# RMSNorm with GELU: tiles taken one at a time in a hand-written order, half of the squares moved from ScalarE to VectorE

One core of one Trainium2 chip. The metric is the device time of one execution in microseconds, median of the fast runs. All runs in this study were in the fast state, with a granted clock of 1.00 in each.

## The reference

`x` is 8 x 1024 x 2048 float32, `gamma` has 2048 elements. Every row is normalised, scaled and passed through GELU:

```python
rms = np.sqrt(np.mean(x ** 2, axis=-1, keepdims=True) + eps)
out = gamma * x / rms
return 0.5 * out * (1 + np.tanh(np.sqrt(2 / np.pi) * (out + 0.044715 * out ** 3)))
```

67.1 MB have to come in and 67.1 MB have to go out. There are 32 tiles of 256 rows (128 partitions x 2 rows x 2048), 2.1 MB each way.

## The kernel before

Loads are issued by SyncE, stores by ScalarE's queue. For a group of two tiles ScalarE squares and sums each row into `ssq`, VectorE multiplies by gamma into a bf16 tile `w`; then VectorE works out 1/rms for the group by a bit trick and two Newton steps (10 small operations); then ScalarE applies GELU with 1/rms as its scale.

```python
SG = 2                                             # tiles in a group
xpool = tc.tile_pool(name="xpool", bufs=5)         # (cut: enter_context)
wpool = tc.tile_pool(name="wpool", bufs=4)
ypool = tc.tile_pool(name="ypool", bufs=3)
sqpool = tc.tile_pool(name="sqpool", bufs=2, space=PSUM)
...
for G in group_sizes:
    for j in range(G):
        nc.sync.dma_start(out=x_tile, in_=...)
        for t in range(T):
            nc.scalar.activation(out=sq_scratch, in_=x_tile[:, t, :], func=AF.Square,
                                 accum_out=ssq[:, j * T + t: j * T + t + 1])
        nc.vector.tensor_mul(out=w_tile, in0=x_tile, in1=gamma_bc)
    # 10 small VectorE operations on 128 x 4: ssq -> mtile -> ... -> rr
    for j in range(G):
        for t in range(T):
            nc.scalar.activation(out=y_tile[:, t, :], in_=w_tiles[j][:, t, :],
                                 func=AF.Gelu_apprx_tanh, scale=rr[:, ...])
        nc.scalar.dma_start(out=..., in_=y_tile)
```

The order in which VectorE and ScalarE issue these is not the order written. A scheduler in the framework places them, and in the built program VectorE's multiplies stand ahead of the statistics: the multiply of tile 31 (290.34 us in the trace), for one, stands before the statistics of tiles 28 and 29 (294.68 us), so that four multiplied tiles (the four `w` buffers) wait for theirs. "Statistics" here are the small operations that make 1/rms. This order turns out to matter more than which engine does the squares.

Of the kernel before, what the change touches and what calls it, by code (L numbers as in the profile page):

```python
# [1 line left out]

# [4 lines left out]

FP32 = mybir.dt.float32
BF16 = mybir.dt.bfloat16
I32 = mybir.dt.int32  # L10
AF = mybir.ActivationFunctionType
ALU = mybir.AluOpType

_RSQRT_MAGIC = float(0x5F3759DF)


@with_exitstack
def kernel(
    ctx: ExitStack,
    tc: tile.TileContext,  # L20
    x: bass.AP,
    gamma: bass.AP,
    eps: float,
    out: bass.AP,
):
    nc = tc.nc
    P = nc.NUM_PARTITIONS

    xf = x.flatten_outer_dims()
    of = out.flatten_outer_dims()  # L30
    N, H = xf.shape

    T = 2
    rows_per_tile = P * T
    assert N % rows_per_tile == 0
    ntiles = N // rows_per_tile
    SG = 2
    COLS = SG * T

    singles = ctx.enter_context(tc.tile_pool(name="singles", bufs=1))  # L40
    xpool = ctx.enter_context(tc.tile_pool(name="xpool", bufs=5))
    wpool = ctx.enter_context(tc.tile_pool(name="wpool", bufs=4))
    ypool = ctx.enter_context(tc.tile_pool(name="ypool", bufs=3))
    sqpool = ctx.enter_context(tc.tile_pool(name="sqpool", bufs=2, space=bass.MemoryType.PSUM))
    stats = ctx.enter_context(tc.tile_pool(name="stats", bufs=4))

    gamma_sb = singles.tile([P, H], FP32)
    nc.sync.dma_start(out=gamma_sb, in_=gamma.partition_broadcast(P))
    gamma_bc = gamma_sb.rearrange("p (o h) -> p o h", o=1).to_broadcast([P, T, H])

    inv_h = 1.0 / float(H)
    eps_f = float(eps)

    group_sizes = [SG] * (ntiles // SG)
    rem = ntiles % SG
    if rem:
        group_sizes.append(rem)

    base = 0
    for G in group_sizes:  # L60
        ssq = stats.tile([P, COLS], FP32)
        mtile = stats.tile([P, COLS], FP32)
        y0i = stats.tile([P, COLS], I32)
        t0 = stats.tile([P, COLS], FP32)
        t1 = stats.tile([P, COLS], FP32)
        u0 = stats.tile([P, COLS], FP32)
        y1 = stats.tile([P, COLS], FP32)
        t2 = stats.tile([P, COLS], FP32)
        t3 = stats.tile([P, COLS], FP32)
        u1 = stats.tile([P, COLS], FP32)  # L70
        rr = stats.tile([P, COLS], FP32)

        ncols = G * T
        w_tiles = []
        for j in range(G):
            i = base + j
            r0 = i * rows_per_tile
            x_tile = xpool.tile([P, T, H], FP32)
            nc.sync.dma_start(
                out=x_tile,  # L80
                in_=xf[r0:r0 + rows_per_tile, :].rearrange("(p t) h -> p t h", t=T),
            )

            for t in range(T):
                sq_scratch = sqpool.tile([P, H], FP32)
                nc.scalar.activation(  # L86
                    out=sq_scratch,
                    in_=x_tile[:, t, :],
                    func=AF.Square,
                    accum_out=ssq[:, j * T + t: j * T + t + 1],  # L90
                )

            w_tile = wpool.tile([P, T, H], BF16)
            nc.vector.tensor_mul(out=w_tile, in0=x_tile, in1=gamma_bc)  # L94
            w_tiles.append(w_tile)

        sg = slice(0, ncols)
        nc.vector.tensor_scalar(  # L98
            out=mtile[:, sg], in0=ssq[:, sg], scalar1=inv_h, scalar2=eps_f,
            op0=ALU.mult, op1=ALU.add,  # L100
        )
        nc.vector.tensor_scalar(  # L102
            out=y0i[:, sg], in0=mtile[:, sg].bitcast(I32), scalar1=-0.5,
            scalar2=_RSQRT_MAGIC,
            op0=ALU.mult, op1=ALU.add,
        )
        y0f = y0i.bitcast(FP32)
        nc.vector.tensor_mul(out=t0[:, sg], in0=y0f[:, sg], in1=y0f[:, sg])  # L108
        nc.vector.tensor_mul(out=t1[:, sg], in0=t0[:, sg], in1=mtile[:, sg])  # L109
        nc.vector.tensor_scalar(  # L110
            out=u0[:, sg], in0=t1[:, sg], scalar1=-0.5, scalar2=1.5,
            op0=ALU.mult, op1=ALU.add,
        )
        nc.vector.tensor_mul(out=y1[:, sg], in0=y0f[:, sg], in1=u0[:, sg])  # L114
        nc.vector.tensor_mul(out=t2[:, sg], in0=y1[:, sg], in1=y1[:, sg])  # L115
        nc.vector.tensor_mul(out=t3[:, sg], in0=t2[:, sg], in1=mtile[:, sg])  # L116
        nc.vector.tensor_scalar(  # L117
            out=u1[:, sg], in0=t3[:, sg], scalar1=-0.5, scalar2=1.5,
            op0=ALU.mult, op1=ALU.add,
        )  # L120
        nc.vector.tensor_mul(out=rr[:, sg], in0=y1[:, sg], in1=u1[:, sg])  # L121

        for j in range(G):
            i = base + j
            r0 = i * rows_per_tile
            y_tile = ypool.tile([P, T, H], FP32)
            for t in range(T):
                nc.scalar.activation(  # L128
                    out=y_tile[:, t, :],
                    in_=w_tiles[j][:, t, :],  # L130
                    func=AF.Gelu_apprx_tanh,
                    scale=rr[:, j * T + t: j * T + t + 1],
                )
            nc.scalar.dma_start(
                out=of[r0:r0 + rows_per_tile, :].rearrange("(p t) h -> p t h", t=T),
                in_=y_tile,
            )

        base += G


# [1 line left out]
_INS = ['x', 'gamma', 'eps']  # L143
_OUTS = [((8, 1024, 2048), 'float32')]
#: Inputs that are plain numbers.
_NUMBERS = {'eps': 9.999999747378752e-06}


# [26 lines left out]
```

## Time and profile before

| | before |
|---|---|
| median | 330.06 us (329.39 to 330.27, 13 runs) |
| span of the profiled run | 328.0 us |
| VectorE / ScalarE busy | 166.5 us (51%) / 247.0 us (75%) |
| moved | 135.3 MB, 412 GB/s over the span |
| moved in the middle (100 to 256 us, four windows of 39 us) | 430 to 432 GB/s |
| transfers idle in the tail (the two "holes") | 3.0 + 5.5 us |

The busy shares are averages over the span. The rate in the middle against the rate over the span tells more: something is lost outside the middle. The lines are in the prediction.

### The profile page before, as it was taken

The page shows a single profiled execution, that of the slowest core. Times are in us where ns is not written, and L with a number is a line of the kernel's source. Part 1 is how long each engine was busy: PE and PEld are TensorE (multiplying, and loading weights), DVE is VectorE, ACT ScalarE, POOL GpSimd, SP SyncE. Part 2 cuts the span into 40 slices and gives each one's busy share as a digit, 9 for nine tenths or more (in the row PEclk, how much of TensorE's full clock was granted, in tenths as well). Part 3 has the DMA queues.
Part 4 walks back from the last instruction along what each step waited for, and adds up shares of the span by engine and source line. Part 5 has one row for each costly group of instructions (what it writes and reads, how often), then busy time and mean ns, then how long its engine had stood idle before and what let it go on. Part 6 is the DMA issues. An engine that isn't in the chain of part 4 may idle for free.

```text
span 328.0 us, 586 instructions
## 1 busy us (share of the span) xinstructions
DVE 166.5 (51%) x192; ACT 247.0 (75%) x194; POOL 0.2 (0%) x4
## 2 busy tenths in 40 slices
DVE  0698476557544365654447554455754446551100
ACT  1589719996976949589594977949498694968890
POOL 0000000000000000000000000000000000000000
DMA  8999999999999999999999999999999999996938
GB/s 314 438 424 372 428 434 428 436 428 437 424 440 421 440 424 440 424 438 426 438 426 438 426 438 424 436 426 436 427 436 428 434 428 433 430 434 262 388 160 352
DMA packets 9364, 135.30 MB, mean 412 GB/s; under 512 B 1040, under 2 KB 1040, under 8 KB 1040
## 3 DMA queue, kind: packets, MB, share of 16 engines
q1 hardware_dynamic: 4752, 68.16, 49.1%
q10 hardware_dynamic: 4608, 67.11, 47.8%
q14 instruction: 4, 0.03, 0.0%
HBM read 68.16 MB, written 67.11 MB: 412 GB/s over the span
## 4 chain that ended last, share of the span: by engine, by line
DMA 43%; ACT 24%; DVE 19%; issue 12%; SPq 0%; DVEq 0%
DMA x_tile<-in_x_dram 37%; ACT y_tile L128 19%; DVE w_tile L94 13%; DMA out_dram<-y_tile 6%; ACT sq_scratch L86 5%; DVE u L117 1%; DVE y0i L102 1%; DVE u L110 1%; DVE t L108 1%; DVE t L116 1%; DVE y L114 1%; DVE rr L121 1%; DVE t L109 1%; DVE t L115 1%; DVE mtile L98 0%
## 5 line engine op out<-in xcount | busy, mean ns | idle before, releaser
L94 DVE TENSOR_TENSOR w_tile<-x_tile,gamma_sb 128x4096 bf16<-128x4096 f32 x32 | 141.4, 4425 | 126.4 <-DMA x_tile<-in_x_dram 58.4
L128 ACT ACTIVATE y_tile<-w_tile,rr 128x2048 f32<-128x2048 bf16 x64 | 123.1, 1991 | 62.5 <-DVE rr L121 62.1
L86 ACT ACTIVATE sq_scratch<-x_tile 128x2048 f32<-128x2048 f32 x64 | 118.9, 1858 | 9.5 <-DMA x_tile<-in_x_dram 9.5
L86 ACT ACTIVATION_READ_ACCUMULATOR sq_scratch<-x_tile 128x1 f32 x64 | 11.9, 186 | 0.0
L98 DVE TENSOR_SCALAR mtile<-ssq 128x4 f32<-128x4 f32 x16 | 2.6, 164 | 14.1 <-ACT sq_scratch L86 14.1
L117 DVE TENSOR_SCALAR u<-t 128x4 f32<-128x4 f32 x16 | 2.7, 170 | 0.6
L110 DVE TENSOR_SCALAR u<-t 128x4 f32<-128x4 f32 x16 | 2.7, 170 | 0.6
L102 DVE TENSOR_SCALAR y0i<-mtile 128x4 int32<-128x4 int32 x16 | 2.7, 170 | 0.5
L108 DVE TENSOR_TENSOR t<-y0i 128x4 f32<-128x4 f32 x16 | 2.6, 163 | 0.5
L109 DVE TENSOR_TENSOR t<-t,mtile 128x4 f32<-128x4 f32 x16 | 2.6, 162 | 0.5
L116 DVE TENSOR_TENSOR t<-t,mtile 128x4 f32<-128x4 f32 x16 | 2.6, 162 | 0.6
L115 DVE TENSOR_TENSOR t<-y 128x4 f32<-128x4 f32 x16 | 2.6, 161 | 0.6
L114 DVE TENSOR_TENSOR y<-y0i,u 128x4 f32<-128x4 f32 x16 | 2.6, 162 | 0.5
L121 DVE TENSOR_TENSOR rr<-y,u 128x4 f32<-128x4 f32 x16 | 2.6, 161 | 0.5
L86 ACT ACT_TABLE_LOAD x1 | 1.3, 1283 | 0.7 <-PEq L156 0.7
L128 ACT ACT_TABLE_LOAD x1 | 1.3, 1283 | 0.0
L156 POOL MEMSET const-uint8-127<- 128x1 uint8 x1 | 0.1, 103 | 0.0
L156 POOL MEMSET const-bfloat16-1.0<- 128x1 bf16 x1 | 0.1, 102 | 0.0
L156 POOL MEMSET const-float32-0.0<- 128x1 f32 x1 | 0.1, 99 | 0.2 <-issue 0.2
L156 POOL MEMSET const-float32-1.0<- 128x1 f32 x1 | 0.1, 99 | 0.0
## 6 DMA issues: line engine op xcount, KB each, us to landing
x_tile<-in_x_dram SPq DMA_DIRECT2D x32, 2048.0 KB, 23.5
out_dram<-y_tile ACTq DMA_DIRECT2D x32, 2048.0 KB, 19.3
gamma_sb<-in_gamma_dram SPq DMA_DIRECT2D x1, 1024.0 KB, 4.8
```

The costliest lines, as they stand in the source:

```text
L86: nc.scalar.activation(out=sq_scratch, in_=x_tile[:, t, :], func=AF.Square, accum_out=ssq[:, j * T + t: j * T + t + 1],)
L94: nc.vector.tensor_mul(out=w_tile, in0=x_tile, in1=gamma_bc)
L102: nc.vector.tensor_scalar(out=y0i[:, sg], in0=mtile[:, sg].bitcast(I32), scalar1=-0.5, scalar2=_RSQRT_MAGIC, op0=ALU.mult, op1=ALU.add,)
L108: nc.vector.tensor_mul(out=t0[:, sg], in0=y0f[:, sg], in1=y0f[:, sg])
L109: nc.vector.tensor_mul(out=t1[:, sg], in0=t0[:, sg], in1=mtile[:, sg])
L110: nc.vector.tensor_scalar(out=u0[:, sg], in0=t1[:, sg], scalar1=-0.5, scalar2=1.5, op0=ALU.mult, op1=ALU.add,)
L114: nc.vector.tensor_mul(out=y1[:, sg], in0=y0f[:, sg], in1=u0[:, sg])
L115: nc.vector.tensor_mul(out=t2[:, sg], in0=y1[:, sg], in1=y1[:, sg])
L116: nc.vector.tensor_mul(out=t3[:, sg], in0=t2[:, sg], in1=mtile[:, sg])
L117: nc.vector.tensor_scalar(out=u1[:, sg], in0=t3[:, sg], scalar1=-0.5, scalar2=1.5, op0=ALU.mult, op1=ALU.add,)
L121: nc.vector.tensor_mul(out=rr[:, sg], in0=y1[:, sg], in1=u1[:, sg])
L128: nc.scalar.activation(out=y_tile[:, t, :], in_=w_tiles[j][:, t, :], func=AF.Gelu_apprx_tanh, scale=rr[:, j * T + t: j * T + t + 1],)
```

## The change

Its intent is to balance the two engines and shorten the path of a tile. One of a tile's two rows of squares goes to VectorE as a fused multiply-and-sum; tiles are handled one at a time; one Newton step goes; there are four y buffers for three; and a hand order replaces the scheduler's on VectorE and ScalarE, with the next tile's square ahead of this tile's GELUs. The core, with cuts:

```diff
-    SG = 2
-    COLS = SG * T
+    COLS = 2
-    ypool = ... bufs=3      sqpool = ... bufs=2
+    ypool = ... bufs=4      sqpool = ... bufs=1
+    # DVE and ACT issue in the order written here.
+    ctx.enter_context(tc.manual_schedule(
+        engines={mybir.EngineType.DVE, mybir.EngineType.Activation}))
+    def front(i):                                   # (cut: load, tiles)
+        nc.vector.tensor_tensor_reduce(
+            out=dve_sq_scratch, in0=x_tile[:, 0, :], in1=x_tile[:, 0, :],
+            scale=inv_h, scalar=eps_f, op0=ALU.mult, op1=ALU.add, accum_out=m[:, 0:1])
+        nc.scalar.activation(out=act_sq_scratch, in_=x_tile[:, 1, :], func=AF.Square,
+                             scale=sqrt_inv_h, accum_out=s)
+        nc.vector.tensor_mul(out=w, in0=x_tile, in1=gamma_bc)
+        ...                                         # 6 small operations on 128 x 2 (10 on 128 x 4 before)
+    def back(i):
+        for t in range(T):
+            nc.scalar.activation(out=y[:, t, :], in_=ws[i][:, t, :],
+                                 func=AF.Gelu_apprx_tanh, scale=rrs[i][:, t:t + 1])
+        nc.scalar.dma_start(out=o, in_=y)
+    for i in range(ntiles):
+        front(i)
+        if i:
+            back(i - 1)
+    back(ntiles - 1)
```

More of the change, by code (lines that the diff above doesn't have):

```diff
@@ L34 @@
     rows_per_tile = P * T
-    assert N % rows_per_tile == 0
     ntiles = N // rows_per_tile
-    SG = 2
-    COLS = SG * T
+    COLS = 2
     singles = ctx.enter_context(tc.tile_pool(name="singles", bufs=1))
@@ L42 @@
     wpool = ctx.enter_context(tc.tile_pool(name="wpool", bufs=4))
-    ypool = ctx.enter_context(tc.tile_pool(name="ypool", bufs=3))
-    sqpool = ctx.enter_context(tc.tile_pool(name="sqpool", bufs=2, space=bass.MemoryType.PSUM))
+    ypool = ctx.enter_context(tc.tile_pool(name="ypool", bufs=4))
+    sqpool = ctx.enter_context(tc.tile_pool(name="sqpool", bufs=1, space=bass.MemoryType.PSUM))
     stats = ctx.enter_context(tc.tile_pool(name="stats", bufs=4))
@@ L51 @@
     inv_h = 1.0 / float(H)
+    sqrt_inv_h = float(inv_h ** 0.5)
     eps_f = float(eps)
-    group_sizes = [SG] * (ntiles // SG)
-    rem = ntiles % SG
-    if rem:
-        group_sizes.append(rem)
-    base = 0
-    for G in group_sizes:
-        ssq = stats.tile([P, COLS], FP32)
-        mtile = stats.tile([P, COLS], FP32)
-        y0i = stats.tile([P, COLS], I32)
-        t0 = stats.tile([P, COLS], FP32)
-        t1 = stats.tile([P, COLS], FP32)
-        u0 = stats.tile([P, COLS], FP32)
-        y1 = stats.tile([P, COLS], FP32)
-        t2 = stats.tile([P, COLS], FP32)
-        t3 = stats.tile([P, COLS], FP32)
-        u1 = stats.tile([P, COLS], FP32)
-        rr = stats.tile([P, COLS], FP32)
-        ncols = G * T
-        w_tiles = []
-        for j in range(G):
-            i = base + j
-            r0 = i * rows_per_tile
-            x_tile = xpool.tile([P, T, H], FP32)
-            nc.sync.dma_start(
-                out=x_tile,
-                in_=xf[r0:r0 + rows_per_tile, :].rearrange("(p t) h -> p t h", t=T),
-            )
-            for t in range(T):
-                sq_scratch = sqpool.tile([P, H], FP32)
-                nc.scalar.activation(
-                    out=sq_scratch,
-                    in_=x_tile[:, t, :],
-                    func=AF.Square,
-                    accum_out=ssq[:, j * T + t: j * T + t + 1],
-                )
-            w_tile = wpool.tile([P, T, H], BF16)
-            nc.vector.tensor_mul(out=w_tile, in0=x_tile, in1=gamma_bc)
-            w_tiles.append(w_tile)
-        sg = slice(0, ncols)
-        nc.vector.tensor_scalar(
-            out=mtile[:, sg], in0=ssq[:, sg], scalar1=inv_h, scalar2=eps_f,
-            op0=ALU.mult, op1=ALU.add,
-        )
-        nc.vector.tensor_scalar(
-            out=y0i[:, sg], in0=mtile[:, sg].bitcast(I32), scalar1=-0.5,
-            scalar2=_RSQRT_MAGIC,
-            op0=ALU.mult, op1=ALU.add,
-        )
-        y0f = y0i.bitcast(FP32)
-        nc.vector.tensor_mul(out=t0[:, sg], in0=y0f[:, sg], in1=y0f[:, sg])
-        nc.vector.tensor_mul(out=t1[:, sg], in0=t0[:, sg], in1=mtile[:, sg])
-        nc.vector.tensor_scalar(
-            out=u0[:, sg], in0=t1[:, sg], scalar1=-0.5, scalar2=1.5,
-            op0=ALU.mult, op1=ALU.add,
-        )
-        nc.vector.tensor_mul(out=y1[:, sg], in0=y0f[:, sg], in1=u0[:, sg])
-        nc.vector.tensor_mul(out=t2[:, sg], in0=y1[:, sg], in1=y1[:, sg])
-        nc.vector.tensor_mul(out=t3[:, sg], in0=t2[:, sg], in1=mtile[:, sg])
-        nc.vector.tensor_scalar(
-            out=u1[:, sg], in0=t3[:, sg], scalar1=-0.5, scalar2=1.5,
-            op0=ALU.mult, op1=ALU.add,
-        )
-        nc.vector.tensor_mul(out=rr[:, sg], in0=y1[:, sg], in1=u1[:, sg])
-        for j in range(G):
-            i = base + j
-            r0 = i * rows_per_tile
-            y_tile = ypool.tile([P, T, H], FP32)
-            for t in range(T):
-                nc.scalar.activation(
-                    out=y_tile[:, t, :],
-                    in_=w_tiles[j][:, t, :],
-                    func=AF.Gelu_apprx_tanh,
-                    scale=rr[:, j * T + t: j * T + t + 1],
-                )
-            nc.scalar.dma_start(
-                out=of[r0:r0 + rows_per_tile, :].rearrange("(p t) h -> p t h", t=T),
-                in_=y_tile,
-            )
-        base += G
@@ new lines, with rows @@
+    act_sq_scratch = sqpool.tile([P, H], FP32)
+    dve_sq_scratch = singles.tile([P, H], FP32)
+    ctx.enter_context(tc.manual_schedule(
+        engines={mybir.EngineType.DVE, mybir.EngineType.Activation}))
+    xs, ws, rrs = {}, {}, {}
+    def rows(i):
+        return slice(i * rows_per_tile, (i + 1) * rows_per_tile)
+    def front(i):
+        x_tile = xpool.tile([P, T, H], FP32, name="x_tile")
+        nc.sync.dma_start(out=x_tile, in_=xf[rows(i), :].rearrange("(p t) h -> p t h", t=T))
+        m = stats.tile([P, COLS], FP32, name="mtile")
+        s = stats.tile([P, 1], FP32, name="s_act")
+        nc.vector.tensor_tensor_reduce(
[3 more added lines that the diff above has]
+                             scale=sqrt_inv_h, accum_out=s)
+        w = wpool.tile([P, T, H], BF16, name="w_tile")
+        nc.vector.tensor_mul(out=w, in0=x_tile, in1=gamma_bc)
+        y0i = stats.tile([P, COLS], I32, name="y0i")
+        t0 = stats.tile([P, COLS], FP32, name="t0")
+        t1 = stats.tile([P, COLS], FP32, name="t1")
+        u0 = stats.tile([P, COLS], FP32, name="u0")
+        rr = stats.tile([P, COLS], FP32, name="rr")
+        nc.vector.tensor_scalar(out=m[:, 1:2], in0=s, scalar1=eps_f, scalar2=None, op0=ALU.add)
+        nc.vector.tensor_scalar(out=y0i, in0=m.bitcast(I32), scalar1=-0.5,
+                                scalar2=_RSQRT_MAGIC, op0=ALU.mult, op1=ALU.add)
+        y0f = y0i.bitcast(FP32)
+        nc.vector.tensor_mul(out=t0, in0=y0f, in1=y0f)
+        nc.vector.tensor_mul(out=t1, in0=t0, in1=m)
+        nc.vector.tensor_scalar(out=u0, in0=t1, scalar1=-0.5, scalar2=1.5, op0=ALU.mult, op1=ALU.add)
+        nc.vector.tensor_mul(out=rr, in0=y0f, in1=u0)
+        ws[i], rrs[i] = w, rr
@@ L143 @@
+    def back(i):
+        y = ypool.tile([P, T, H], FP32, name="y_tile")
+        o = of[rows(i), :].rearrange("(p t) h -> p t h", t=T)
+        for t in range(T):
+            nc.scalar.activation(out=y[:, t, :], in_=ws[i][:, t, :], func=AF.Gelu_apprx_tanh,
+                                 scale=rrs[i][:, t:t + 1])
+        nc.scalar.dma_start(out=o, in_=y)
[4 more added lines that the diff above has]
+    back(ntiles - 1)
 _INS = ['x', 'gamma', 'eps']
```

## The prediction

> **What bounds the kernel now.** I read the page from the top: busy time of each engine, then the slices, then the costly rows.
>
> ```profile
> DVE 166.5 (51%) x192; ACT 247.0 (75%) x194; POOL 0.2 (0%) x4
> ...
> DVE  0698476557544365654447554455754446551100
> ACT  1589719996976949589594977949498694968890
> ...
> DMA  8999999999999999999999999999999999996938
> GB/s 314 438 424 372 428 434 428 436 428 437 424 440 421 440 424 440 424 438 426 438 426 438 426 438 424 436 426 436 427 436 428 434 428 433 430 434 262 388 160 352
> ```
>
> No compute engine is full: ScalarE is busy 75% of the span, VectorE 51%. The DMA line is at 9 in every slice from the second to the 36th and drops only in the last four (6, 9, 3, 8; the span is 328.0 us, so a slice is 8.2 us). So the kernel has two stages: some 298 us in which the transfers are the limit, and a tail in which they wait for work. The three large groups:
>
> ```profile
> L94 DVE TENSOR_TENSOR w_tile<-x_tile,gamma_sb 128x4096 bf16<-128x4096 f32 x32 | 141.4, 4425 | 126.4 <-DMA x_tile<-in_x_dram 58.4
> L128 ACT ACTIVATE y_tile<-w_tile,rr 128x2048 f32<-128x2048 bf16 x64 | 123.1, 1991 | 62.5 <-DVE rr L121 62.1
> L86 ACT ACTIVATE sq_scratch<-x_tile 128x2048 f32<-128x2048 f32 x64 | 118.9, 1858 | 9.5 <-DMA x_tile<-in_x_dram 9.5
> ```
>
> ScalarE's 62 us of waiting for `rr` look tempting, but they lie in the stage in which the transfers never pause, so they cost nothing there. What the transfers leave unused is read from the windows of the tail (length, busy time of DVE, ACT and POOL, clock, DMA share, GB/s):
>
> ```profile
> 296.00:298.00 2.00, 0.53 (x4) 1.33 (x1) 0.00 (x0) 1.00 0.82 352
> 298.00:300.00 2.00, 0.00 (x0) 2.00 (x2) 0.00 (x0) 1.00 0.06 25
> 300.00:302.00 2.00, 0.00 (x0) 2.00 (x2) 0.00 (x0) 1.00 0.31 131
> 302.00:304.00 2.00, 0.00 (x0) 2.00 (x2) 0.00 (x0) 1.00 1.15 483
> ...
> 310.00:312.00 2.00, 1.64 (x10) 0.02 (x1) 0.00 (x0) 1.00 0.62 262
> 312.00:314.00 2.00, 0.01 (x1) 1.96 (x2) 0.00 (x0) 1.00 0.00 0
> 314.00:316.00 2.00, 0.00 (x0) 2.00 (x3) 0.00 (x0) 1.00 0.00 0
> 316.00:318.00 2.00, 0.00 (x0) 2.00 (x2) 0.00 (x0) 1.00 0.61 262
> ```
>
> With one-microsecond windows the edges are about 298.1 to 301.1 and 311.0 to 316.5: two holes, 3.0 and 5.5 us, 8.5 us in all, and ScalarE busy in nearly all of both. The timeline says why: groups of two tiles. The last group's statistics come only after all its squares on ScalarE, which stand behind the previous group's GELUs.
>
> ```profile
> 300.59 0.34 ACTq L134 DMA_DIRECT2D out_dram<-y_tile  x1
> ...
> 310.05 0.17 DVE L98 TENSOR_SCALAR mtile<-ssq 128x4 f32<-128x4 f32 x1 [13.42 <-ACT sq_scratch L86]
> ...
> 312.04 5.79 ACT L128 ACTIVATE y_tile<-w_tile,rr 128x2048 f32<-128x2048 bf16 x3 [2.02 <-DVE rr L121]
> 315.97 0.34 ACTq L134 DMA_DIRECT2D out_dram<-y_tile  x1
> ```
>
> The last input tile is multiplied from 290.34 us on and the program ends at 328.0, so about 38 us follow the last load.
>
> [...] in the middle, groups of two tiles start their GELUs at 140.24 and 159.67 us, 19.43 us apart, in which 4 x 2.097 MB = 8.39 MB move, 432 GB/s. So I expect nothing from the middle. [...] loads alone land 4.9 us apart (multiplies released at 10.51 and 15.33), beside stores 9.7 us apart (31.82 and 41.55). [...]
>
> **The change part by part.**
> - *Squares.* Half of the 64 squares leave ScalarE: 32 x (1858 + 186 - 93 overlap) ns, some 62 us. VectorE gets 32 fused multiply-and-sum operations of 2048 elements[...].
> - *Statistics.* 10 small operations per two tiles become 6 per tile, so 12 per two; they start 0.20 us apart in the timeline, so 1.2 us per tile. One Newton step goes; that is accuracy, not time.
> - *VectorE per tile*: 2.3 + 0.1 + 4.4 + 1.2 = 8.0 us. *ScalarE per tile*: 1.95 (square) + 3.9 (two GELUs at 1.9 us from start to start) + about 1 for issuing the store before the next square = 7. Both lie under the 9.7 us that the transfers need per tile, so the middle stays bound by the transfers, with 1.7 us of room on VectorE.
> - *Order.* square(i+1) stands before gelu(i) on ScalarE, so a store is issued about 16 us after its tile landed: 9.7 until the next lands, 2.0 square, 3.9 GELU, 0.1. The group of two is gone.
> - *Buffers.* Four y tiles for three. gelu(i) needs store(i-4) done; I count below that it is, by over 10 us. The PSUM scratch has one buffer; it is written by ScalarE alone, in order.
>
> Now the whole run. Tile 0 lands at 10.4 as before. VectorE: to 12.9 sum, 17.3 multiply, 18.5 statistics. ScalarE: square(0), square(1) to 17.3, table load 1.3, gelu(0) 18.7 to 22.6, store issued 22.7 (it was 25.59), data moving from an estimated 23.5. By then 1 + (23.5 - 10.4)/4.88 = 3.7 tiles are loaded: the loads lead the stores by 3.7 tiles. VectorE makes a tile every 8.0 us and a store takes 9.7 beside a load, so the store queue does not run dry, and with both queues full and equal shares the lead stays 3.7. Store k then runs from 23.5 + 9.72k, and the last load lands at T = 23.5 + (32 - 3.7) x 9.72 = 298.6. (gelu(i) starts at about 9 + 9.72i, store(i-4) ends at 23.5 + 9.72(i-3) = -6 + 9.72i: 15 us to spare.)
>
> Tail, from T: 3.7 stores are left; alone each takes 5.0 us (two took 301.1 to 311.0). Stores 28 and 29, already issued, run to T+8.5. Store 30: square(31) 2.0, gelu(30) 3.9, issued T+6.1, in time; it runs to T+13.5. Store 31: VectorE 8.0, gelu(31) 4.0, issued T+12.1, moving T+12.9, just in time; ends T+18.5. The old run ends 1.4 us after the last byte (326.6 to 328.0), so the span is 298.6 + 18.5 + 1.4 = 318.5. A second way: the old transfers were active from 2.1 to 326.6 less 8.5, 316.0 us; with no hole at all 2.1 + 316.0 + 1.4 = 319.5. The median is 2.1 us above the span, so 320.6 to 321.6; I take 321.2, which is 2.7% off.
>
> **The rivals.**
> - *VectorE becomes the bound.* [...] it takes about 4.4 us instead of 2.3, a tile 10.1, over the 9.7 of the transfers: 10.4 + 32 x 10.1 + gelu 4.0 + store 5.8 + 1.4 = 345 span, 347 us, slower by 5%. [...] About 6%.
> - *The hole closes only in part.* The tail has only 0.5 us of slack before store 31. A dispatch gap behind each store issue, or a store queue that ran dry in the middle so that the loads got further ahead (the old lead at the last load was about 5.5 tiles), leaves 2 to 4 us of idle: 323 to 325. For it: the old run did let its loads get ahead. Against it: the holes came of work in groups, and at T only one square and four GELUs are left. About 20%.
> - *Nothing gained*, as ScalarE's relief was hidden behind transfers anyway: right for the middle, and about 330 if the tail stayed. I see no way for the tail to stay whole.
> - *More than that.* The dip to 372 GB/s in the fourth slice (a loss of 8.2 x 60/430 = 1.1 us) may go as well, since x tiles are freed by one square and come back earlier: 319 to 320.
>
> **Range and chances.** The 2% line is 323.5 us, 2.3 above my estimate; the two workings differ by 1. The range is 319.0 to 324.5: below it a better rate than this trace has in the middle would be needed, above it a hole of over 3 us or a busy VectorE. Faster by over 2% 0.74; within 2% 0.19, nearly all from the partly closed hole; slower 0.07, the first rival.
>
> **What would show it.** Right: DMA at 9 up to the last slice but one; the new sum at about 2.3 us; VectorE near 245 us busy (141 + 77 + 31), ScalarE near 187; first store issued at 22 to 23 us; last load landing near 299, 20 us before the end; 430 GB/s in the middle. Wrong: a sum of 4 us or more with VectorE at 9 throughout; holes in the last three slices; or a middle rate that changed.

Where its figures come from: the 2.3 us for the new sum is an estimate, and a straight line through the two-tensor operations in the trace of the kernel before, 162 ns for 4 elements and 4425 for 4096, gives the same: 2291 ns for 2048. That the new sum would lie on this line, the 0.1 us for reading its accumulator (77 us in all for 32 sums with their reads) and the 1 us for issuing a store before the next square were the author's estimates, which no trace had shown. The 4.4 us of the first rival was assumed as well. That the middle has no more to give is read from the rates: loads alone move 2.097 MB in 4.82 us, 435 GB/s, and loads with stores 432; that nothing faster is possible was not shown.

## The result and the profile after

The changed kernel takes 321.59 us (321.41 to 321.86, 8 runs) against 330.06: ratio 0.9746, interval 0.9737 to 0.9756. Ratios here and below are the mean time of one kernel's fast runs over that of the kernel before in the same rounds, so not quite the ratio of the medians quoted.

The page of the changed kernel, busy times and the 40 slices (8.0 us each):

```profile
DVE 240.1 (75%) x288; ACT 188.6 (59%) x130; POOL 0.2 (0%) x4
...
DVE  0699999998777797777887768877778877779710
ACT  1398777477555577555676545765556764557740
...
DMA  8999999999999999999999999999999999999996
GB/s 314 430 430 385 432 430 429 426 426 435 437 431 430 430 426 428 439 430 435 432 426 426 437 431 430 430 430 430 428 437 432 432 430 428 426 432 437 431 430 279
```

VectorE and ScalarE have changed places (75% and 59%), and that is not where the time came from. The DMA line is: it stays at 9 to the last slice but one. In the middle nothing changed: 430 to 432 GB/s in the same four windows. The dip in the fourth slice is still there (372 GB/s before, 385 now), so the prediction's rival "more than that" did not come. The large groups:

```profile
L74 DVE TENSOR_TENSOR w_tile<-x_tile,gamma_sb 128x4096 bf16<-128x4096 f32 x32 | 141.5, 4421 | 0.0
L94 ACT ACTIVATE y_tile<-w_tile,rr 128x2048 f32<-128x2048 bf16 x64 | 124.2, 1988 | 6.8 <-DVE rr L87 6.8
L71 ACT ACTIVATE act_sq_scratch<-x_tile 128x2048 f32<-128x2048 f32 x32 | 60.2, 1882 | 113.2 <-DMA x_tile<-in_x_dram 111.5
L68 DVE CUSTOM_DVE_ANT_0 dve_sq_scratch<-x_tile 128x2048 f32<-128x2048 f32 x32 | 73.3, 2291 | 59.8 <-DMA x_tile<-in_x_dram 59.8
```

The new sum takes 2291 ns for 2048 elements, both operands the same row of `x` (about 2.3 us were predicted; two different rows were not run), and the read of its accumulator 83 ns. Both engines now wait for loads, 111.5 and 59.8 us: the thing that bounds the kernel. ScalarE's 62 us of waits for `rr` have shrunk to 6.8. The timeline of the last tile, from its landing to the last store's issue, and the windows of the tail (columns as in the prediction):

```profile
297.72 2.29 DVE L68 CUSTOM_DVE_ANT_0 dve_sq_scratch<-x_tile 128x2048 f32<-128x2048 f32 x1 [2.02 <-DMA x_tile<-in_x_dram]
...
303.54 0.34 ACTq L96 DMA_DIRECT2D out_dram<-y_tile  x1
...
309.37 0.34 ACTq L96 DMA_DIRECT2D out_dram<-y_tile  x1
```

```profile
300.00:302.00 2.00, 2.00 (x3) 2.00 (x2) 0.00 (x0) 1.00 1.02 438
...
308.00:310.00 2.00, 0.00 (x0) 1.34 (x1) 0.00 (x0) 1.00 1.03 442
310.00:312.00 2.00, 0.00 (x0) 0.00 (x0) 0.00 (x0) 1.00 0.95 410
```

The last load lands at 297.7 (at about 290 before), and 22 us follow it instead of 38. The last store is issued 11.7 us after that landing, while the transfers are still busy with the stores queued ahead. The two holes, 8.5 us, are gone, and the span fell by 8.2.

### The profile page after: what moved, and what is told of

Read it like the earlier page. It is cut to its first block, busy times and chain, and to the rows that moved or that the text cites. A ratio compares the mean times of both kernels' runs of the same rounds, so it can differ in the third digit from the quotient of the medians.

```text
span 319.8 us, 593 instructions
## 1 busy us (share of the span) xinstructions
DVE 240.1 (75%) x288; ACT 188.6 (59%) x130; POOL 0.2 (0%) x4
## 4 chain that ended last, share of the span: by engine, by line
DMA 76%; DVE 19%; ACT 1%; issue 0%; SPq 0%
DMA x_tile<-in_x_dram 76%; DVE w_tile L74 11%; DVE dve_sq_scratch L68 6%; ACT y_tile L94 1%; DVE u L86 0%; DVE y0i L81 0%; DVE t L85 0%; DVE t L84 0%; DVE rr L87 0%; DVE mtile L80 0%; SPq L46 0%; SPq L65 0%; DVE mtile L68 0%
## 5 line engine op out<-in xcount | busy, mean ns | idle before, releaser
L71 ACT ACTIVATE act_sq_scratch<-x_tile 128x2048 f32<-128x2048 f32 x32 | 60.2, 1882 | 113.2 <-DMA x_tile<-in_x_dram 111.5
L68 DVE CUSTOM_DVE_ANT_0 dve_sq_scratch<-x_tile 128x2048 f32<-128x2048 f32 x32 | 73.3, 2291 | 59.8 <-DMA x_tile<-in_x_dram 59.8
L86 DVE TENSOR_SCALAR u<-t 128x2 f32<-128x2 f32 x32 | 5.4, 169 | 1.1
L81 DVE TENSOR_SCALAR y0i<-mtile 128x2 int32<-128x2 int32 x32 | 5.4, 169 | 1.1
L85 DVE TENSOR_TENSOR t<-t,mtile 128x2 f32<-128x2 f32 x32 | 5.2, 161 | 1.1
L71 ACT ACTIVATION_READ_ACCUMULATOR act_sq_scratch<-x_tile 128x1 f32 x32 | 6.0, 187 | 0.0
L87 DVE TENSOR_TENSOR rr<-y0i,u 128x2 f32<-128x2 f32 x32 | 5.1, 161 | 1.1
L84 DVE TENSOR_TENSOR t<-y0i 128x2 f32<-128x2 f32 x32 | 5.1, 160 | 1.1
L80 DVE TENSOR_SCALAR mtile<-s_act 128x1 f32<-128x1 f32 x32 | 4.7, 146 | 0.0
L68 DVE DVE_READ_ACCUMULATOR2_ANT mtile<- 128x1 f32 x32 | 2.6, 83 | 0.0
## 6 DMA issues: line engine op xcount, KB each, us to landing
out_dram<-y_tile ACTq DMA_DIRECT2D x32, 2048.0 KB, 26.8
```

The costliest lines, as they stand in the source:

```text
L68: nc.vector.tensor_tensor_reduce(out=dve_sq_scratch, in0=x_tile[:, 0, :], in1=x_tile[:, 0, :], scale=inv_h, scalar=eps_f, op0=ALU.mult, op ...
L71: nc.scalar.activation(out=act_sq_scratch, in_=x_tile[:, 1, :], func=AF.Square, scale=sqrt_inv_h, accum_out=s)
L80: nc.vector.tensor_scalar(out=m[:, 1:2], in0=s, scalar1=eps_f, scalar2=None, op0=ALU.add)
L81: nc.vector.tensor_scalar(out=y0i, in0=m.bitcast(I32), scalar1=-0.5, scalar2=_RSQRT_MAGIC, op0=ALU.mult, op1=ALU.add)
L84: nc.vector.tensor_mul(out=t0, in0=y0f, in1=y0f)
L85: nc.vector.tensor_mul(out=t1, in0=t0, in1=m)
```

## The experiments

All kernels gave the reference's result. A verdict of faster or slower asks for 2%; smaller differences below are read from the ratios and their intervals. The table has each one beside the kernel before of the same rounds; "gone" means that no hole is left before the last store.

| label | differs from | median us | ratio to before | 95% interval | holes in the tail |
|---|---|---|---|---|---|
| (the change) | | 321.59 | 0.9746 | 0.9737 to 0.9756 | gone |
| groups_of_one | before | 347.24 | 1.0529 | 1.0512 to 1.0546 | (another bound) |
| split_squares | before | 334.19 | 1.0128 | 1.0104 to 1.0152 | one of 11 us |
| last_groups | before | 331.24 | 1.0042 | 1.0026 to 1.0058 | three |
| one_newton | before | 327.69 | 0.9933 | 0.9914 to 0.9953 | two, shorter |
| written_order | before | 326.39 | 0.9898 | 0.9879 to 0.9917 | one of 5.4 us |
| written_y_four | before | 321.75 | 0.9753 | 0.9739 to 0.9768 | gone |
| act_squares | change | 322.05 | 0.9768 | 0.9745 to 0.9790 | gone |
| auto_order | change | 323.81 | 0.9820 | 0.9801 to 0.9839 | several short |
| no_lookahead | change | 321.93 | 0.9758 | 0.9743 to 0.9773 | gone |
| order_only | change | 323.04 | 0.9790 | 0.9773 to 0.9807 | gone |
| dve_plus_full | change | 340.97 | 1.0339 | 1.0318 to 1.0359 | (another bound) |
| gamma_onchip | change | 320.09 | 0.9706 | 0.9687 to 0.9726 | gone |

### Parts of the change laid on the kernel before

**groups_of_one**

```diff
-    SG = 2
+    SG = 1
```

> The kernel before with groups of one tile instead of two; squares stay all on ScalarE, two Newton steps, the scheduler's own order. Theory 1 (the gain is the tail: what stands between the last load and the last stores): after the last load ScalarE has about one and a half squares, four GELUs and one chain of statistics left, so store 31 moves about 14 us after the last load while 3 stores (15 us) are still in the queue; the holes close and the median is 321.5 to 323.5 us. Theory 2 (the gain comes from moving half the squares to VectorE, because ScalarE at 9.1 of 9.7 us per tile cannot keep up): the time stays at 328 to 331 us. Both say 430 to 434 GB/s in the middle.

Measured: 347.24 us. Both theories were wrong, and this was the most instructive run. The waits and a stretch of the timeline:

```profile
DVE w_tile L94 <- ACT y_tile L128: 97.1, 25, 4.0
```

```profile
158.94 4.42 DVE L94 TENSOR_TENSOR w_tile<-x_tile,gamma_sb 128x4096 bf16<-128x4096 f32 x1 [3.96 <-ACT y_tile L128]
...
163.28 0.16 DVE L98 TENSOR_SCALAR mtile<-ssq 128x2 f32<-128x2 f32 x1
...
165.25 3.89 ACT L128 ACTIVATE y_tile<-w_tile,rr 128x2048 f32<-128x2048 bf16 x2 [0.67 <-DVE rr L121]
...
169.18 4.42 DVE L94 TENSOR_TENSOR w_tile<-x_tile,gamma_sb 128x4096 bf16<-128x4096 f32 x1 [3.96 <-ACT y_tile L128]
```

The multiply waits for GELUs to free its `w` buffer; the statistics of the tile three before it stand behind that multiply on VectorE; the GELUs wait for these statistics; and the next multiply waits for these GELUs. That is a closed loop between two engines: 4.3 + 2.0 + 3.9, 10.24 us from multiply to multiply. The transfers need 9.7 per tile, so the loop, not the transfers, now bounds the kernel, with no engine over 72% busy. With groups of two the same loop carries two tiles: in the kernel before, from 144.16 to 163.59 us, it holds 14.7 us of work (multiplies of 4.4 and 4.3, 2.0, 3.9) and 4.75 of waiting for a load, so the loads, at 19.4 per two tiles, set its pace. So this order, with its multiplies three tiles ahead, needs the group. It does not hold for every order that the scheduler makes: auto_order, below, goes tile by tile too and has no such loop.

**split_squares**

```diff
+            # (cut: the tile dve_sq_scratch)
+            nc.vector.tensor_tensor_reduce(out=dve_sq_scratch, in0=x_tile[:, 0, :], in1=x_tile[:, 0, :],
+                scale=1.0, scalar=0.0, op0=ALU.mult, op1=ALU.add, accum_out=ssq[:, j * T: j * T + 1])
-            for t in range(T):
+            for t in range(1, T):
```

> The kernel before with the first square of each tile on VectorE as in the change, groups still of two, two Newton steps, the scheduler's own order. Theory 1: the last group's statistics stand behind the last tile's sum and multiply (2.3 + 4.4 + 2.0 us), store 30 is issued some 13 us and store 31 some 17 us after the last load; ScalarE has time to issue stores 28 and 29 at about the last load, so a hole of 0 to 3.5 us is left: 321.5 to 325 us. Theory 2: the whole gain, 321 to 322 us. A third, that the grouping alone is the cause: 328 to 331 us.

Measured: 334.19 us, slower than before, against all three. The timeline near the last load:

```profile
291.22 2.29 DVE L85 CUSTOM_DVE_ANT_0 dve_sq_scratch<-x_tile 128x2048 f32<-128x2048 f32 x1 [6.80 <-DMA x_tile<-in_x_dram]
...
295.42 5.79 ACT L133 ACTIVATE y_tile<-w_tile,rr 128x2048 f32<-128x2048 bf16 x3 [12.43 <-DVE rr L126]
...
299.35 0.34 ACTq L139 DMA_DIRECT2D out_dram<-y_tile  x1
```

In the built order the sum of a late tile stands ahead of two finished groups' statistics. VectorE waits 6.8 us for that tile's load, ScalarE 12.4 us for the statistics behind it, and the transfers stand still from about 289 to 300 us. Moving the squares adds one more operation that waits for a load to VectorE's queue; by itself, in the order that the scheduler then made, it did not help.

**last_groups**

```diff
-    group_sizes = [SG] * (ntiles // SG)
+    group_sizes = [SG] * (ntiles // SG - 1) + [1, 1]
```

> The kernel before with its last group of two split into two groups of one, nothing else. If the size of the last group alone makes the tail: about 325 us, as store 30 no longer waits for tile 31's squares. Theory 1 in detail says no gain: the first hole ends with the statistics of tiles 28 and 29, which stand on VectorE behind the multiply of tile 31 as before, and ScalarE, not the group, is then the bound: GELUs 28 and 29 to 304, a square, statistics, GELU 30 to 312, two squares to 316, statistics, GELU 31 to 322, store to 328 to 329: 328.5 to 331.5 us.

Measured: 331.24 us, as the detailed working had it. The first hole is where it was (windows from 298 to 301 us), and the second is split in two by ScalarE's backlog of squares. Making the last group smaller is not enough.

**one_newton**

```diff
-        (y1, t2, t3, u1: four small operations)
-        nc.vector.tensor_mul(out=rr, in0=y1, in1=u1)
+        nc.vector.tensor_mul(out=rr, in0=y0f, in1=u0)
```

> The kernel before with one Newton step instead of two (6 small operations per group instead of 10), nothing else. Theory 1: the chain of the tail holds two groups' statistics, each 0.8 us shorter, and nothing else changes: 1.6 us less, 328.0 to 329.0 us. If the statistics were hidden throughout: 330.1 us. If the middle gained as well (16 groups x 0.8 us): 317 us.

Measured: 327.69 us, 2.1 us less; 1.6 was worked out. The transfer-share windows show the two holes at about 1.4 and 4.7 us instead of 3.0 and 5.5. A few 0.2 us operations count for nothing in the middle (16 groups x 0.8 us would have been 12.8) and fully in the tail, where both groups' statistics are on the path. In the change itself the step can hardly count, since written_y_four and order_only, below, have no hole with both steps; the change with two steps was not run.

### The order by itself

**written_order**

```diff
+    ctx.enter_context(tc.manual_schedule(
+        engines={mybir.EngineType.DVE, mybir.EngineType.Activation}))
```

> The kernel before with one line added: VectorE and ScalarE issue in the order written, so that a group's statistics stand directly behind that group's own multiplies. Nothing else of the change (groups of two, all squares on ScalarE, two Newton steps, three y buffers). Theory 3, formed after the first four runs (the scheduler's order put statistics behind multiplies or sums of tiles up to four later, so a store waited for a later load; the hand order is what pays): the whole gain. ScalarE per two tiles 7.6 squares + 2.2 wait for statistics + 7.7 GELUs + 0.8 = 18.3 us, under 19.4; last load at about 296 us, store 30 moving 10.8 us and store 31 about 14.3 us after it, with stores queued for 11.5 us: no hole, 320.5 to 323 us. Theory 2 (moved squares): about 330 us. If all parts are needed together: 325 us or more.

Measured: 326.39 us: 3.5 of the 8.5 us, so theory 3 as stated was too strong. The first hole is gone; one of 5.4 us is left, from about 307.4 to 312.8. The waits name what is left, and the windows show the hole:

```profile
ACT y_tile L131 <- DMA out_dram<-y_tile: 16.5, 11, 1.9
```

```profile
308.00:310.00 2.00, 0.30 (x2) 1.63 (x1) 0.00 (x0) 1.00 0.04 16
310.00:312.00 2.00, 0.00 (x0) 2.00 (x2) 0.00 (x0) 1.00 0.00 0
```

ScalarE waits 11 times, up to 1.9 us, for a store to free a y buffer. With 18.3 us of its own per two tiles (in the trace, 19.8 from the GELUs at 288.57 to those at 308.37 us, less the 1.5 that such a wait added) in a period of 19.4 it has no room for that, so its last squares are late.

**written_y_four**

```diff
 (written_order, and)
-    ypool = ctx.enter_context(tc.tile_pool(name="ypool", bufs=3))
+    ypool = ctx.enter_context(tc.tile_pool(name="ypool", bufs=4))
```

> The one-line order change to the kernel before, plus a fourth y buffer. In that run ScalarE waited 1.5 to 1.9 us per group for a store to free a y buffer, which with 18.3 us of its own per group fills the whole period of 19.4, so that its last squares lagged the loads by some 12 us and one hole of 5 us was left. If these waits cause the hole: ScalarE catches up with the loads by 1.1 us per group, the hole closes, 321.5 to 323 us. If the group of two is the cause: 325.5 to 326.5 us as with three buffers.

Measured: 321.75 us, ratio 0.9753, whose interval overlaps that of the change (0.9746). The page's DMA slices:

```profile
DMA  8999999999999999999999999999999999999996
```

So the kernel before plus two small edits, an order directive and one more buffer, gets the whole gain with its groups of two, all its squares on ScalarE and both Newton steps. So order and buffer suffice, and grouping and balance are not needed with them. A fourth y buffer under the scheduler's order was not run; in the trace of the kernel before a GELU waits for a store to free a y buffer only once, for 0.3 us, so little is to be expected of it there.

### Parts of the change taken back

**act_squares**

```diff
-        nc.vector.tensor_tensor_reduce(out=dve_sq_scratch, ..., accum_out=m[:, 0:1])
-        nc.scalar.activation(out=act_sq_scratch, in_=x_tile[:, 1, :], ..., accum_out=s)
+        for t in range(T):
+            nc.scalar.activation(out=act_sq_scratch, in_=x_tile[:, t, :], func=AF.Square,
+                                 scale=sqrt_inv_h, accum_out=s[:, t:t + 1])
 (cut: tiles and the first small operation, to match)
```

> The changed kernel with both squares of a tile back on ScalarE and no sum on VectorE; hand order, tile by tile. ScalarE 3.8 + 3.9 + 0.4 = 8.1 us per tile, VectorE 5.6. Theory 3: no loss, 321 to 322.5 us: the two holes stay closed, since store 31 is issued about 12 us after the last load as in the change. Theory 2: the gain is lost, 327 us or more.

Measured: 322.05 us. With ScalarE back at 79% and VectorE at 53% the time is the same within what these runs tell apart (0.9768 against 0.9746, intervals overlap). Moving 62 us of squares is worth 0.5 us by the medians and 0.7 by the ratios, neither clear of the noise.

**auto_order**

```diff
-    ctx.enter_context(tc.manual_schedule(
-        engines={mybir.EngineType.DVE, mybir.EngineType.Activation}))
```

> The changed kernel without its hand order: the scheduler places the instructions of VectorE and ScalarE. In the built program the last operation of tile 27's statistics stands behind the sum of tile 31, and the statistics of 28 to 31 behind that. Theory 3: the statistics run three to four loads late, about 5.75 stores are left at the last load, with some 4 to 5 us of holes: 323 to 328 us, VectorE's or ScalarE's waits for the other much longer than in the change. If order does not matter: 321.6 us.

Measured: 323.81 us. All else of the change kept, the scheduler's order costs 2.2 us: ScalarE waits 107.8 us for `rr` instead of 6.8, and the transfer share drops in several windows between 292 and 310 us. Order matters in both kernels, more so in the one before (3.5 us by written_order). But the run also says that the hand order is not the only way: under the scheduler's order the rest of the change keeps 6.1 of its 8.5 us by the medians. Here the multiplies stand only two tiles ahead (the multiply of tile 30, at 288.63 us, before the statistics of tile 28), and no multiply waits for a GELU, as it did for 97.1 us in groups_of_one. Which of the other parts (squares, Newton step, y buffer, or the order that the scheduler makes of them) brings this was not separated.

**no_lookahead**

```diff
     for i in range(ntiles):
         front(i)
-        if i:
-            back(i - 1)
-    back(ntiles - 1)
+        back(i)
```

> The changed kernel with each tile's GELUs directly behind its own square, without the next tile's square in between. ScalarE per tile: square 1.95, wait for statistics 1.4, GELUs 3.9, store issue 0.4 = 7.7 us, under 9.7; a store is issued about 11.5 us after its load instead of 16, but the transfers are full either way: 321.3 to 322 us, no change. If the square ahead is what closes the holes: 324 us or more.

Measured: 321.93 us, no change to speak of. ScalarE now waits 95.6 us for `rr` and the transfers do not notice. The square ahead is not needed.

**order_only**

```diff
 (act_squares, and)
-    ypool ... bufs=4
+    ypool ... bufs=3
+    (the second Newton step: y1, t2, t3, u1)
```

> The changed kernel with everything undone but the order: tile by tile, hand order, square of the next tile ahead of the GELU of this one; both squares on ScalarE, two Newton steps, three y buffers, as the kernel before has them. If the order (tile by tile, statistics behind their own multiply, one square ahead) is the whole cause: 321.5 to 322.5 us, no hole in the tail, 8.2 us per tile on ScalarE, 6.6 on VectorE. If the moved squares, the single Newton step or the fourth y buffer are needed with it: 324 us or more.

Measured: 323.04 us (322.52 to 323.39), between the two expectations; against the 2% line the verdict is unclear (0.9773 to 0.9807). Its profiled run, a fast one of 322.52 us, has a span of 320.4 us and no hole. Its waits:

```profile
ACT y_tile L99 <- DMA out_dram<-y_tile: 26.6, 19, 2.0
```

With three buffers the wait for stores is back, 19 times, and is nearly harmless because ScalarE has more room here than in written_order: 8.35 us of its own in the 9.72 of a tile (from the GELUs at 156.74 to those at 166.46 us, less the 1.37 that such a wait added), against 18.3 in the 19.4 of two tiles. Against act_squares, run in another call, 0.7 us stays by the ratios, and the intervals overlap; against written_y_four and no_lookahead, run in the same call with four y buffers, it is 1.3 and 1.1 us. Whether the buffer or the Newton step makes it was not separated.

### The rival bound, and a faster version

**dve_plus_full**

```diff
 (the change, and behind each sum)
+        nc.vector.tensor_tensor(out=dve_sq_scratch, in0=x_tile[:, 0, :], in1=gamma_sb, op=ALU.mult)
```

> The changed kernel with one more fp32 multiply of 2048 elements (2.2 us, result unused) behind each sum on VectorE: the prediction's first rival made real. VectorE 7.6 + 2.2 = 9.8 us per tile, just over the 9.7 of the transfers. If VectorE then bounds the run from the first load on: 10.6 + 32 x 9.8 + GELU 4.0 + store 5.8 + 2.4 = 336 us span, 338 us. If only what is over 9.7 per tile counts (32 x 0.1): 325 us. If VectorE does not matter: 321.6 us. The result of the kernel is unchanged.

Measured: 340.97 us. The slices of VectorE and of the transfers:

```profile
DVE  0799999999999999999999999999999999999960
...
DMA  8999999999999999999999999999999999944455
```

The first rival of the prediction was real in size, only not in fact. A period of 9.92 us on VectorE (multiplies start at 153.77 and 163.69), just 0.2 over what the transfers need, costs 19 us, not 32 x 0.2 = 6. The transfers still run at 9 for 34 slices, but it is the loads that get ahead: VectorE waits for a load only once, for the first (10.2 us); at the end only stores are left to move, as fast as VectorE works off the tiles loaded ahead. When one engine bounds from the first load on, its whole work plus the head and the last tile's path is the time: 10.6 + 32 x 9.92 + 4.0 + 5.8 + 2.2 = 340.0, where the span was 339.1. Setting this sum to the change's span of 319.8 gives 9.3 us per tile: an estimate of where VectorE would begin to show, against 7.6 that it has.

**gamma_onchip**

```diff
-    nc.sync.dma_start(out=gamma_sb, in_=gamma.partition_broadcast(P))
+    # (cut: the tiles gamma_row, ones_row, gamma_ps)
+    nc.sync.dma_start(out=gamma_row, in_=gamma.rearrange("(o h) -> o h", o=1))
+    nc.vector.memset(ones_row, 1.0)
+    for c in range(0, H, 512):
+        nc.tensor.matmul(out=gamma_ps[:, c:c + 512], lhsT=ones_row,
+                         rhs=gamma_row[:, c:c + 512], start=True, stop=True)
+    nc.vector.tensor_copy(out=gamma_sb, in_=gamma_ps)
```

> A version meant to beat both kernels: the changed kernel with gamma loaded once as one row of 8 KB and spread to the partitions on chip (four matmuls with a row of ones into PSUM, one copy by VectorE) instead of a 1 MB broadcast load. If the changed kernel is bound by the bytes moved from the first load to the last store, 1.05 MB less at 431 GB/s is 2.4 us less: 319.2 us. If its start hides the broadcast, or its tail is set by the engines: 321.6 us.

Measured: 320.09 us, the fastest here; 321.75 and 321.93 for the kernels of the same chip and call that keep the broadcast. The span is 318.1 against 319.8. The gain is 1.7 us, not 2.4: the first load's square starts at 8.94 instead of 10.59 us, 1.65 us sooner. The missing 0.7 us stands in the windows of the head: up to 10 us this version moved 3.06 MB and the change 3.36, and 0.30 MB at 431 GB/s are 0.7 us. Its transfers come up more slowly (238 GB/s from 2 to 4 us, against 307), so not all of the 1.05 MB turned into time; why they do, I did not test. That fewer bytes give less time, where moving 62 us of engine work gave nothing to speak of, is what a transfer-bound kernel should show.

## Why the prediction was right, point by point

- **What bounds the kernel** held: middle unchanged, two holes in the tail worth 8.5 us, span down by 8.2.
- **The walk through the run** held closely. First store issued at 22.7 reckoned, 22.80 measured; last load at 298.6, 297.7; store 30 issued 6.1 us after it, 5.8; store 31 12.1, 11.7; stores left at that point 3.7, 3.95 (8.3 MB in the window from 297.72 on); end after the last byte 1.4, about 1.9. Span 318.5 to 319.5 reckoned, 319.8 measured: the walk's own 318.5 was 1.3 short, from a last load 0.9 sooner, stores that took 1.7 longer and an end 0.5 longer. The rival of a hole closed only in part did not come: store 31 had some 2.7 us of slack where 0.5 was reckoned (an estimate: the last bytes moved at about 317.9 us, and the time from its issue at 309.37, less 5.0 for the store itself and 0.8 from issue to first byte, is 2.7; in the kernel before, the store issued at 300.59 moved its first bytes at 301.4, the one at 315.97 at 316.8). Loads alone were 4.82 us apart by the two lines that the prediction names, not 4.9, which changes little.
- **Costs of operations** held: the sum 2.29 us plus 0.08; VectorE 7.6 per tile, from the multiply at 20.41 us to that at 28.01 (8.0 reckoned; operations that follow each other overlap: the sum that starts at 10.59 lasts 2.29, to 12.88, and the multiply behind it starts at 12.80); ScalarE 188.6 busy (187); a store issue before the next square 0.41 to 0.45 us (about 1). VectorE was 240.1 busy; the prediction wrote 245, though its terms, 141 + 77 + 31, add to 249, and the page's groups add to 248, with overlaps.
- **The first rival** was given 6%, and its 4.4 us for the sum did not come (2291 ns measured); that it would not was a guess that came out. dve_plus_full, at 340.97 us, shows that the stake (347 us) was of the right size.
- **A step that was mis-sized**: "gelu(i) needs store(i-4) done; ... 15 us to spare". In the trace gelu(15) starts at 153.03 us, and store(11) lands some 4.7 us later than its reckoned end, judging by store 15, which was reckoned to end at 179.0 and landed 26.8 us (the median of the page's issue table) after its issue at 156.94. That leaves about 8, less than the 9.7 of one tile, so with one buffer fewer a GELU would have to wait some 1.5 us: in order_only it does, 19 times, 26.6 us in all.
- **A reading that failed**: ScalarE's waits for `rr` "cost nothing there". For the waits in the middle that fits, since the transfers never paused; but they are the sign of statistics that come late, and the one of 4.45 us that ends at 296.67 stands right before the first hole.
- **A step of the explanation that failed**: the prediction put the holes down to "groups of two" and expected the tile-by-tile form to close them. Groups of one under the scheduler's order are 5.3% slower; groups of two in the written order with four y buffers get all. What counts is the order, with buffers enough for it: in the kernel before, statistics of finished tiles stood behind operations that waited for later loads. (By auto_order it is not the only thing that can close most of the holes.) The prediction listed the hand order as one part among others and gave it no time of its own, nor the fourth buffer; its number was right because its walk used both throughout.

The first hole in the kernel before shows the step, and written_y_four, with the same groups, what the order changes. Before, the squares of tiles 28 and 29 are done at 290.33 us, but their statistics stand behind the multiply of tile 31, which cannot start before load 31 lands, at about 290.2 (issued at 266.74, 23.5 us to landing; the view names a square that ended at the same moment):

```profile
290.34 4.43 DVE L94 TENSOR_TENSOR w_tile<-x_tile,gamma_sb 128x4096 bf16<-128x4096 f32 x1 [5.27 <-ACT sq_scratch L86]
...
294.68 0.16 DVE L98 TENSOR_SCALAR mtile<-ssq 128x4 f32<-128x4 f32 x1
...
296.67 5.79 ACT L128 ACTIVATE y_tile<-w_tile,rr 128x2048 f32<-128x2048 bf16 x3 [4.45 <-DVE rr L121]
```

That is 4.3 us, where the hole is 3.0. The second hole follows: ScalarE, idle until then, has three squares left behind the four GELUs, and the last statistics wait for them until 310.05 us. In written_y_four the statistics of tiles 28 and 29 stand before the multiply of tile 30:

```profile
279.70 0.16 DVE L101 TENSOR_SCALAR mtile<-ssq 128x4 f32<-128x4 f32 x1
...
285.79 4.42 DVE L97 TENSOR_TENSOR w_tile<-x_tile,gamma_sb 128x4096 bf16<-128x4096 f32 x1 [4.13 <-DMA x_tile<-in_x_dram]
```

## What to carry to other kernels

When the transfers run full in the middle, look at what follows the last load before you balance the engines: a store can be late because its inputs stand, in some engine's order, behind an operation that waits for a later load. Check the built order, not the written one, and try an order directive and one more output buffer before any rewriting; here these two small edits did what the whole rewrite did. After that, of what was tried here, only fewer bytes helped (1.7 us, gamma_onchip).
